# Joining pairs of groups in the routed stage of a hybrid attention and expert-retrieval block, with a rearranged front

## The chip, the cores and the metric

One core of one Trainium2 chip runs the whole layer as one launch. The metric is the time of one execution on the device in microseconds (us); lower is better. The engines are named as in the profile: PE is TensorE (matrix products), PEld its weight loads, DVE is VectorE, ACT ScalarE, POOL GpSimd and SP SyncE, which issues most DMAs. Matrix products write only to PSUM, a memory of eight banks of 512 float32 columns by 128 rows; the other tiles lie in SBUF.

## The reference

Sequence 256, model width 2048, all float32. Cut to what matters:

```python
h = x @ w_in[l]                                    # q, six k/v, gates, conv
kc, vc = compress_kv(k_c, ...), compress_kv(v_c, ...)   # 15 compressed positions
p_c = masked_softmax(q @ kc * scale - slopes * dist_c)  # "compressed scores"
o_nsa = g0 * (p_c @ vc) + g1 * o_slc + g2 * o_win       # gated branches
x = layer_norm(ALPHA * x + concat(o_nsa, o_conv) @ w_out)
# PEER: 8 heads, product keys 128 x 128 = 16384 experts
s1, s2 = q1 @ keys1, q2 @ keys2                    # per token and head
v1, i1 = top_k(s1, 16); v2, i2 = top_k(s2, 16)
top, pos = top_k(v1[:, None] + v2[None, :], 16)    # 16 of 256 candidates
eidx = i1[pos // 16] * 128 + i2[pos % 16]; g = softmax(top)
hid = gelu(sum_d(y * u_tab[eidx]))                 # 128 experts per token
out = layer_norm(ALPHA * y + sum(g * hid * v_tab[eidx]))
```

With n_slc = 4 blocks and 16 to select, all causal blocks are selected, so the selected branch is plain causal attention over all 256 positions.

## The kernel before

The kernel has five stages, and TensorE works through nearly all of them.

1. **Front.** `w_in`, `w_out` and `wq` are streamed as pieces of 1 MB (`add_piece`, `run`). Each piece is handled as two halves; each half is split into a high part `hi` (a cast on ScalarE, `high_to`, line 228) and a low part `lo` (a subtraction on VectorE or GpSimd, `low_to`, line 243), and three products of high and low parts make a float32 product (`mm3`, lines 281 to 283). Parts are made SA = 3 halves ahead of their use. Beside the pieces, generators (`conv_chain`, `compress`, `attend`, `setup_quads`) emit small instructions; a planner's clock, estimated from costs written in the code, decides after each piece of products which generator goes on (`advance`). The order is fixed when the program is built; each engine then works in order. `compressed(g)` in `attend` makes the compressed scores of a group of four heads, for the two halves of the sequence (tt) one after the other, in eight small VectorE operations each; `put` transposes them.
2. **Query stage.** For each of the 8 heads, `wq` gives the queries, `wq_keys` the scores, `shortlist` the best 16 on each side (VectorE: max, max_index, match_replace, and a cast of the indices, line 1025), and for the first REARLY = 2 heads `route_steps` joins the sides to 16 of 256 candidates (lines 1034 to 1065). Of each low part of `wq`, 2/8 are made on VectorE and 6/8 on GpSimd (WQDVE = 2).
3. **Dense U stage.** For all 16384 experts the product of the first 1024 columns of `u_tab` with y is made on TensorE and kept in `W` (128 x 256 x 128). For the other 1024 columns only the selected rows are fetched, one gather of 128 rows by GpSimd (line 1104) and one product with sum per 128 (token, expert) pairs (a "dot", line 1115). 56 dots or so are left for the next stage.
4. **Routed stage** (lines 1496 to 1756). The 256 tokens form NQ = 64 groups of four. *Extraction* of a group (`ext_hot`, `ext`, `ext_max`) picks the 128 selected values of each token out of `W`: a small bf16 product of features gives squared distances (`ho`, line 1549), a relu on ScalarE makes them one-hot (`pt`), a second small product writes a mask of -2^100 into a bank (`xp`, line 1557), four float32 products (two records each, line 1559) add the picked rows of W to it, and a maximum on VectorE (line 1564) keeps the value. *Scatter* of a group (`sc_hot`, `sc_val`, `sc`) does the reverse with the gated activations: two small products (`pp`, line 1590), a relu on ScalarE (`oh`, line 1593), a product on VectorE (`oa`, line 1600), four float32 products (`sp`, line 1606) and a copy into `W` on ScalarE (line 1608). The rows of features lie in four ranges of 32 partitions: R1 at 0, RT at 32, RX at 64, R0 at 96. One loop of NQ + LAG = 99 steps runs extraction of group q and scatter of group q - LAG (LAG = 35), written out by hand; so 34 steps have extraction alone, 30 both (the first of them only the scatter's small products), 35 scatter alone. Six PSUM banks serve it: three for small products, two for `xp`, one for `sp`. In the same loop the last gathered rows are dotted: `x_dots` issues as many gathers as a pacing formula allows, VectorE takes two dots of three, and for every third (XPOOL) GpSimd makes the product (line 1668) and ScalarE, two steps later, the sum (line 1678, `x_sum`). `weight_sums`, `weight_gelu`, `weight_gates` and `weight_rows` turn the values of half the tokens into weights, in the middle and at the end.
5. **V stage.** `W`, now the weights, times all of `v_tab` (line 1646 on), with the first 576 columns by gathers; then the second norm.

The loop's extraction step, as it stands:

```python
            if q < NQ:
                ext(q)
                pace = q + 1 + PACE * max(0, q - LAG)
                x_dots(q, min(2 * P, i0 + -(-u_left * pace // (NQ - 4 + PACE * (NQ - 4 - LAG)))))
```

## Time and profile before

| what | us |
|---|---|
| median of 3 runs (1711.64 to 1719.06) | 1715.94 |
| profiled execution, own time | 1719.01 |
| its span, first to last instruction | 1717.2 |
| TensorE busy in it | 1663.4 (97%) |
| VectorE, ScalarE, GpSimd busy | 1480.4, 862.8, 831.4 |
| routed stage, first to last of its products | 182.1 |

The page gives busy time by engine; the queries of the trace cut it into stretches, list waits, and show instructions in order of time. Matmul records overlap, since they are pipelined, so the time from one start to the next says more than a duration. VectorE's busy time contains time in which an instruction was held up after its start. The granted clock of 1.00 stands for full speed.

### The profile page before, as it was taken

The page shows a single profiled execution, that of the slowest core. Times are in us where ns is not written, and L with a number is a line of the kernel's source. Part 1 is how long each engine was busy: PE and PEld are TensorE (multiplying, and loading weights), DVE is VectorE, ACT ScalarE, POOL GpSimd, SP SyncE. Part 2 cuts the span into 40 slices and gives each one's busy share as a digit, 9 for nine tenths or more (in the row PEclk, how much of TensorE's full clock was granted, in tenths as well). Part 3 has the DMA queues.
Part 4 walks back from the last instruction along what each step waited for, and adds up shares of the span by engine and source line. Part 5 has one row for each costly group of instructions (what it writes and reads, how often), then busy time and mean ns, then how long its engine had stood idle before and what let it go on. Part 6 is the DMA issues. An engine that isn't in the chain of part 4 may idle for free.

```text
span 1717.2 us, 30946 instructions
## 1 busy us (share of the span) xinstructions
PE 1663.4 (97%) x11611; PEld 1513.9 (88%) x11611; DVE 1480.4 (86%) x2763; ACT 862.8 (50%) x1331; POOL 831.4 (48%) x650
## 2 busy tenths in 40 slices
PE   8999999999999999999899999999999999999995
PEld 8998988888999999999899987877888888888884
DVE  6988567756899999999899888865999999999998
ACT  4445666645324444444444546767545555545552
POOL 1874000064663333333333356851766666666664
PEclk9999999999999999999999999999999999999998
DMA  8764435366658999999899987762999999999996
GB/s 273 235 211 138 143 123 173 99 208 190 206 174 309 344 351 347 338 357 348 302 346 355 347 294 220 251 217 73 338 342 341 335 339 347 340 346 339 332 346 238
DMA packets 176592, 470.25 MB, mean 274 GB/s; under 512 B 17891, under 2 KB 85147, under 8 KB 176186
## 3 DMA queue, kind: packets, MB, share of 16 engines
q1 hardware_dynamic: 115680, 257.58, 44.0%
q0 software_dynamic: 57344, 209.75, 34.1%
q8 instruction: 91, 1.49, 0.3%
q10 hardware_dynamic: 3418, 0.94, 0.2%
q14 instruction: 59, 0.48, 0.1%
HBM read 463.36 MB, written 4.85 MB: 273 GB/s over the span
## 4 chain that ended last, share of the span: by engine, by line
PE 69%; DVE 14%; DMA 7%; issue 4%; ACT 3%; POOL 2%; DVEq 0%; SPq 0%; POOLq 0%; ACTq 0%
PE f L282 7%; PE f L281 7%; PE f L283 7%; DMA gv<-in_peer_v_dram,e 5%; PE hp L283 5%; PE hp L281 5%; PE hp L282 5%; PE ut L1171 4%; DVE gu L1115 4%; PE sp L1606 3%; PE xp L1559 3%; DVE ul L1175 2%; DVE lo L243 1%; POOL gu L1104 1%; PE pcg L282 1%
## 5 line engine op out<-in xcount | busy, mean ns | idle before, releaser
L1620 POOL DMA_INDIRECT gv<-in_peer_v_dram,e x256 | 347.7, 1358 | 200.3 <-DVE gacc L1777 154.3
L1104 POOL DMA_INDIRECT gu<-in_peer_u_dram,eu x202 | 193.0, 956 | 330.2 <-DVE gu L1115 245.0
L281 PE MATMUL hp<-yh,uh 128*128 128x256 f32 x1024 | 311.0, 304 | 0.4 <-ACT W L1417 0.3
L282 PE MATMUL f<-vl,wh 128*128 128x512 f32 (+1 forms) x768 | 293.4, 382 | 1.9 <-DVE vl L1646 1.9
L281 PE MATMUL f<-vh,wh 128*128 128x512 f32 (+1 forms) x768 | 294.0, 383 | 0.0
L283 PE MATMUL f<-vh,wl 128*128 128x512 f32 (+1 forms) x768 | 293.0, 382 | 0.0
L283 PE MATMUL hp<-yh,ul 128*128 128x256 f32 x1024 | 290.6, 284 | 0.5 <-DVE ul L1175 0.4
L282 PE MATMUL hp<-yl,uh 128*128 128x256 f32 x1024 | 289.7, 283 | 0.0
L1174 ACT ACTIVATE uh<-ut 128x512 fp32r<-128x512 f32 x256 | 152.7, 598 | 263.5 <-PE ut L1171 257.0
L1646 DVE TENSOR_TENSOR vl<-vr,vh 128x1472 fp32r<-128x1472 f32 x127 | 215.0, 1693 | 33.3 <-ACT vh L1645 33.3
L243 POOL TENSOR_TENSOR lo<-raw,hi 128x1024 fp32r<-128x1024 f32 (+2 forms) x83 | 172.9, 2097 | 129.8 <-ACT hi L228 128.7
L1115 DVE SCALAR_TENSOR_TENSOR gu<-gu,yp 128x1024 f32<-128x1024 f32 x193 | 229.3, 1212 | 2.5 <-DMA gu<-in_peer_u_dram,eu 2.2
L228 ACT ACTIVATE hi<-raw 128x1024 fp32r<-128x1024 f32 (+1 forms) x138 | 142.5, 1037 | 156.8 <-PE pwq L282 41.0
L1634 ACT ACTIVATE wh<-W 128x256 fp32r<-128x256 f32 (+1 forms) x129 | 86.7, 673 | 244.3 <-PE f L282 244.3
L1777 DVE SCALAR_TENSOR_TENSOR gacc<-gv,hv,gacc 128x576 f32<-128x576 f32 x256 | 197.3, 812 | 0.2 <-DMA gv<-in_peer_v_dram,e 0.2
L281 PEld LDWEIGHTS hp<-yh,uh 128*128 128x128 f32 x1024 | 196.5, 192 | 0.8 <-ACT W L1417 0.8
L282 PEld LDWEIGHTS hp<-yl,uh 128*128 128x128 f32 x1024 | 197.1, 192 | 0.0
L283 PEld LDWEIGHTS hp<-yh,ul 128*128 128x128 f32 x1024 | 196.0, 191 | 1.2 <-DVE ul L1175 1.0
L1175 DVE TENSOR_TENSOR ul<-ut,uh 128x512 fp32r<-128x512 f32 x256 | 167.1, 681 | 21.9 <-ACT uh L1174 21.4
L1645 ACT ACTIVATE vh<-vr 128x1472 fp32r<-128x1472 f32 x127 | 180.7, 1423 | 0.0
L282 PEld LDWEIGHTS f<-vl,wh 128*128 128x128 f32 x768 | 144.2, 188 | 26.6 <-DVE vl L1646 2.6
L283 PEld LDWEIGHTS f<-vh,wl 128*128 128x128 f32 x768 | 144.2, 188 | 24.9
(374 smaller groups left out, 3730.4 us busy)
## 6 DMA issues: line engine op xcount, KB each, us to landing
vr<-in_peer_v_dram SPq DMA_DIRECT2D x128, 736.0 KB
ur<-in_peer_u_dram SPq DMA_DIRECT2D x128, 512.0 KB
raw<-in_w_in_dram SPq DMA_DIRECT2D x32, 1024.0 KB
raw<-in_w_out_dram SPq DMA_DIRECT2D x16, 1024.0 KB
raw<-in_peer_wq_dram SPq DMA_DIRECT2D x15, 1024.0 KB
gv<-in_peer_v_dram,e POOLq DMA_INDIRECT x256, 7.0
gu<-in_peer_u_dram,eu POOLq DMA_INDIRECT x202, 7.5
raw<-in_w_in_dram SPq DMA_DIRECT2D x4, 608.0 KB
```

Source lines behind the costliest of these rows:

```text
L243: e.tensor_tensor(lo[:, a:b], src[:, a:b], hi[:, a:b].bitcast(F32), op=OP.subtract)
L281: nc.tensor.matmul(acc, lhsT=ah, rhs=bh, start=start, stop=False)
L282: nc.tensor.matmul(acc, lhsT=ah, rhs=bl, start=False, stop=False)
L283: nc.tensor.matmul(acc, lhsT=al, rhs=bh, start=False, stop=stop)
L1104: nc.gpsimd.indirect_dma_start(out=gt, out_offset=None, in_=ug, in_offset=bass.IndirectOffsetOnAxis(ap=fl(eu, tt)[:, c:c + 1], axis=0))
L1115: nc.vector.scalar_tensor_tensor(gt, gt, 1.0, yr, op0=OP.mult, op1=OP.mult, accum_out=hv[:, tt, c:c + 1])
L1174: nc.scalar.activation(uh, pt, AF.Copy)
L1175: nc.vector.tensor_tensor(ul, pt, uh.bitcast(F32), op=OP.subtract)
L1620: nc.gpsimd.indirect_dma_start(out=gv[:, tt], out_offset=None, in_=v_tab, in_offset=bass.IndirectOffsetOnAxis(ap=fl(e4, tt)[:, j:j + 1], a ...
L1645: nc.scalar.activation(vh, src[:, s], AF.Copy)
L1646: (nc.gpsimd if early else nc.vector).tensor_tensor(vl, src[:, s], vh.bitcast(F32), op=OP.subtract)
L1777: nc.vector.scalar_tensor_tensor(gacc[:, tt], gv[:, tt], wv[:, tt, j:j + 1], gacc[:, tt], op0=OP.mult, op1=OP.add)
```

## The change

It has these parts:

- **Paired groups.** The first QP = 36 groups are extracted in pairs: the small products of two groups are issued together (the second group's from copies of the feature rows at RH = 96 and R1), then their eight float32 products. Then 28 steps with extraction of q and scatter of q - LAG, LAG = 37, and one step with scatter alone; then the last 36 groups are scattered in pairs, with copies of the feature rows at R2 = 32 and RX. The copy of `sp` into W goes to VectorE for every second group of the pairs. Banks and slots are named by hand instead of taken from rings: six banks, and two more in the scatter pairs. The mask's factor 2^100 moves from `quad` into the features. The loads of features, `hot_load` and `feat_load`, are issued once per copy.
- **Casts later.** The cast of the shortlist's indices moves from VectorE to ScalarE, and is issued one head later.
- **One engine per low part.** Of the four halves of a head of `wq`, three low parts are made whole on GpSimd and the fourth on VectorE.
- **Routing in one bank.** For the two early heads the candidates and one-hot products lie in one PSUM bank; ScalarE copies one operand there, and one more reduction writes a copy of i1. The scores of `wq_keys` go round three banks instead of two.
- **Merged compressed scores.** Both halves of the sequence in one set of operations of twice the size; for the first group the banks come from the ring "S".
- **Front.** Low parts are issued after the last `advance` of a half while the planner is in its "quiet" phase (instead of before it), loads of pos and w2 move to the start of `compress`, a guessed cost in `conv_norm` changes, and each next set of compressed scores starts when qT's copy is due.

Cut to what matters:

```diff
-LAGX = 3
+QP = 36
-    taps = const.tile([64, P], BF, name="taps")
-    R1, RT, RX, R0 = slice(0, 20), slice(32, 37), slice(64, 84), slice(96, 116)
+    taps = const.tile([P, P], BF, name="taps")
+    R1, R2, RX, R0 = (slice(a, a + 20) for a in (0, 32, 64, 96))
+    RT, RH = slice(32, 37), slice(96, 101)
...
-                    if j == (len(subs[s]) - 1 if quiet() else len(subs[s]) // 2):
+                    if j == len(subs[s]) // 2 and not quiet():
                         low_to(u + ahead)
                     advance()
+                low_to(u + ahead)
...
+        for nm, pos, w2 in (("k", pos_k, w2_k), ("v", pos_v, w2_v)):
+            w2s[nm] = wk.tile([P, 2, HD], F32, name=f"w2{nm}", tag="w2")
+            nc.scalar.dma_start(w2s[nm], w2[0].rearrange("(c p) d -> p c d", p=P))
+            pns[nm] = wk.tile([16, P], F32, name=f"pn{nm}", tag="pn")
+            nc.scalar.dma_start(pns[nm], pos[0].rearrange("(l r) d -> l (r d)", r=2))
...
+            def begin():
+                c4 = [(psb.tile([P, 512], F32, name=f"cs{g}{half}", tag="S") if g == 0 else turn_tile(f"cs{g}{half}"))
+                      [:, :4 * NCMP].rearrange("p (t h c) -> p t h c", t=2, h=2) for half in range(2)]
...
                 side = compressed(u // per + 1)
+                yield box["qt"]
...
-        add_cols(wq, h * 256, yt, f"pwq{h}", WQDVE if h else 0, lambda a, h=h: accq.__setitem__(h, a))
+        add_cols(wq, h * 256, yt, f"pwq{h}", (0, 0, 0, 8) if h else 0, lambda a, h=h: accq.__setitem__(h, a))
...
-        nc.vector.tensor_copy(f12s[:, :, h], x12)
+        casts[h] = lambda: nc.scalar.activation(f12s[:, :, h], x12, AF.Copy)
...
+        if banked:
+            bank = psb.tile([P, 512], F32, name=f"cand{h}{tt}", tag="T", bufs=1)
+            other = bank[:, T:]
+            cand = flat3(bank, TOPK, TOPK)
+            first = other[:, :TOPK]
+            nc.scalar.activation(first, v12[:, 0], AF.Copy)
+            i1p, efp = (bank[:, i * TOPK:(i + 1) * TOPK] for i in range(2))
+            yield
...
+    def ext_hot(q, pair=False):
+        hp, r = (banks[q % 2], (RT, RH)[q % 2]) if pair else (banks[2], RT)
+        nc.tensor.matmul(hp, lhsT=taps[r], rhs=bts[q // NB][r, :, q % NB], start=True, stop=True)
+        return hp
...
+    def ext_mask(q, pair=False):
+        xps[q], r = (banks[2 + q % 4], (RX, R1)[q % 2]) if pair else (banks[3 + q % 2], RX)
+        nc.tensor.matmul(xps[q], lhsT=frow["ext", q // NB][r, q % NB], rhs=quad[r], start=True, stop=False)
...
+    def sc_hot(m, pair=False):
+        o = 2 * (m % 2) if pair else 0
+        for n, (which, r) in enumerate(((1, R2), (0, RX)) if o else ((1, R1), (0, R0))):
...
+        for q in range(0, QP, 2):
+            loads(q)
+            loads(q + 1)
+            hps_ = [ext_hot(p, True) for p in (q + 2, q + 3)]
+            for p in (q, q + 1):
+                ext_mask(p, True)
+            if q:
+                ext_max(q - 2)
                 ext_max(q - 1)
...
+            for p, hp in zip((q + 2, q + 3), hps_):
+                ext_relu(p, hp, True)
+            for p in (q, q + 1):
+                ext(p)
+                x_dots(p, due(p))
...
+        for m in range(NQ - QP, NQ, 2):
+            loads(m + LAG)
+            loads(m + LAG + 1)
+            nxt = [p for p in (m + 2, m + 3) if p < NQ]
+            for p in nxt:
+                sc_hot(p, True)
+            if m == NQ - QP:
+                weight_gates(1)
+            for p in nxt:
+                sc_relu(p, True)
+            for p in nxt:
+                sc_val(p, True)
+            sps = [sc(p, True) for p in (m, m + 1)]
+            for p, sp in zip((m, m + 1), sps):
+                sc_keep(p, sp, p % 2 == 1)
```

## Rows read from the trace of the kernel before

**Rows 1.** The page, part 1: busy time, share of the span, instructions.

```profile
PE 1663.4 (97%) x11611; PEld 1513.9 (88%) x11611; DVE 1480.4 (86%) x2763; ACT 862.8 (50%) x1331; POOL 831.4 (48%) x650
```

**Rows 2.** Stretches: length, busy by engine (count), granted clock, DMA share, GB/s.

```profile
437.00:510.00 73.00, 69.27 (x567) 68.86 (x566) 71.88 (x253) 23.62 (x25) 49.69 (x30) 0.98 0.57 188
...
1005.60:1055.70 50.10, 49.81 (x344) 36.49 (x343) 39.45 (x65) 28.05 (x49) 34.91 (x30) 1.00 0.79 260
1055.70:1137.90 82.20, 76.21 (x594) 63.05 (x593) 69.72 (x116) 57.90 (x111) 60.57 (x47) 0.94 0.73 236
1137.90:1187.70 49.80, 49.20 (x352) 37.13 (x351) 24.64 (x38) 38.19 (x72) 9.13 (x10) 1.00 0.31 103
```

**Rows 3.** Waits of TensorE: total us, times, longest us.

```profile
PE pwq L283 <- DVE lo L243: 3.2, 1, 3.2
PE ho L1549 <- DVE oa L1600: 2.8, 2, 1.9
PE t L803 <- DVE sc L792: 2.5, 2, 1.4
PE cs L709 <- ACT gates L651: 2.2, 1, 2.2
...
PE ppk L571 <- DMA pnk<-in_cmp_pos_k_dram: 1.7, 1, 1.7
...
PE cs L709 <- ACT qT L662: 0.9, 1, 0.9
```

**Rows 4.** TensorE in order of time, scatter alone: start, duration, instruction.

```profile
1181.26 0.39 PE L1590 MATMUL pp<-quad,fsc 20*128 20x512 bf16 x2
1181.57 1.16 PE L1606 MATMUL sp<-oa,oh 128*128 128x128 f32 x8
1182.66 0.39 PE L1590 MATMUL pp<-quad,fsc 20*128 20x512 bf16 x2
```

**Rows 5.** TensorE in order of time, one joined step of extraction and scatter.

```profile
1068.26 0.39 PE L1590 MATMUL pp<-quad,fsc 20*128 20x512 bf16 x2
1068.27 0.38 PE L1549 MATMUL ho<-bt,taps 5*128 5x512 bf16 x1
1068.27 0.39 PE L1557 MATMUL xp<-quad,fext 20*128 20x512 bf16 x1
1068.59 1.16 PE L1559 MATMUL xp<-W,pt 128*128 128x128 f32 x8
1069.58 1.06 PE L1606 MATMUL sp<-oa,oh 128*128 128x128 f32 x8
1070.57 0.39 PE L1590 MATMUL pp<-quad,fsc 20*128 20x512 bf16 x2
```

**Rows 6.** First and last of 24 joined steps' first small products, 23 periods apart.

```profile
1065.95 0.39 PE L1590 MATMUL pp<-quad,fsc 20*128 20x512 bf16 x2
...
1123.42 0.39 PE L1590 MATMUL pp<-quad,fsc 20*128 20x512 bf16 x2
```

**Rows 7.** A stretch as in rows 2, after the wait for pnk.

```profile
92.00:97.00 5.00, 5.00 (x30) 5.00 (x31) 4.54 (x13) 1.60 (x3) 2.38 (x1) 0.66 0.99 315
```

**Rows 8.** Groups by line on VectorE, 1005.6 to 1137.9: busy us, mean ns, idle before.

```profile
L1564 DVE TENSOR_REDUCE top<-xp 128x4 f32<-128x512 f32 x64 | 44.0, 688 | 11.2 <-PE xp L1559 10.9
L1115 DVE SCALAR_TENSOR_TENSOR spare<-spare,yp 128x1024 f32<-128x1024 f32 x18 | 21.8, 1211 | 1.8 <-DMA spare<-in_peer_u_dram,eu 1.8
```

**Rows 9.** All engines in order of time near 1128; in brackets idle before, releaser.

```profile
1126.54 2.37 POOL L1668 TENSOR_TENSOR moreh<-moreh,morel 128x1024 f32<-128x1024 f32 x1
...
1128.94 1.06 ACT L1678 ACTIVATE moreh<-moreh 128x1024 f32<-128x1024 f32 x1 [2.16 <-POOL moreh L1668]
...
1130.62 1.72 PE L1606 MATMUL sp<-oa,oh 128*128 128x128 f32 x8 [1.69 <-ACT W L1608]
```

**Rows 10.** VectorE and GpSimd in order of time in the query stage, near 470.

```profile
470.00 3.95 DVE L1054 TENSOR_TENSOR oh<-fab,iota 128x256 f32<-128x256 f32 x1
...
470.00 5.66 POOL L243 TENSOR_TENSOR lo<-raw,hi 128x768 fp32r<-128x768 f32 x3
```

More of the change, by code (lines that the diff above doesn't have):

```diff
@@ L434, in setup_quads @@
         yield dv(512, pe(0.43))
-        nc.scalar.dma_start(taps[RT], quad[0:20:4, :P])
+        for r in (RT, RH):
+            nc.scalar.dma_start(taps[r], quad[0:20:4, :P])
         flags.add("quads")
@@ new lines, in compressed, with spread @@
+            sm = wk.tile([P, 2, 2, 4], F32, name=f"csm{g}", tag="csm")
+            box_ = {}
+            def spread(t):
+                return t.rearrange("p t (h o) -> p t h o", o=1).to_broadcast([P, 2, 4, NCMP])
+            def begin():
+                c4 = [(psb.tile([P, 512], F32, name=f"cs{g}{half}", tag="S") if g == 0 else turn_tile(f"cs{g}{half}"))
+                      [:, :4 * NCMP].rearrange("p (t h c) -> p t h c", t=2, h=2) for half in range(2)]
+                for tt in range(2):
+                    for hp_ in range(2):
+                        for half in range(2):
+                            b0 = half * HD
+                            nc.tensor.matmul(c4[half][:, tt, hp_], lhsT=qT[b0:b0 + HD, hp_, tt * P:(tt + 1) * P],
+                                             rhs=kc[b0:b0 + HD, g], start=True, stop=True)
+                t = pe(0.6)
@@ L1039, in route_steps @@
         yield
-        scr = tk.tile([P, T], F32, name=f"scr2{h}{tt}", tag="oh", bufs=1)
+        scr = other if banked else tk.tile([P, T], F32, name=f"scr2{h}{tt}", tag="oh", bufs=1)
         nc.vector.max_index(pos[:, :8], vals[:, :8], src)
@@ L1058, in route_steps @@
             nc.vector.tensor_reduce(dst[:, tt, h], oh, axis=AX.X, op=OP.add)
+            if s == 0 and banked:
+                nc.vector.tensor_reduce(i1p, oh, axis=AX.X, op=OP.add)
             yield
-        ef = tk.tile([P, TOPK], F32, name=f"ef{h}{tt}", tag="ef")
-        nc.vector.scalar_tensor_tensor(ef, i1[:, tt, h], float(P), i2[:, tt, h],
+        ef = efp if banked else tk.tile([P, TOPK], F32, name=f"ef{h}{tt}", tag="ef")
+        nc.vector.scalar_tensor_tensor(ef, i1p, float(P), i2[:, tt, h],
                                        op0=OP.mult, op1=OP.add)
@@ L1373, in tile_hybrid_block @@
         wq_keys(PH - 1, q0)
+        casts[PH - 2]()
         last = scratch(PH - 1)
@@ L1656, in tile_hybrid_block @@
     ups.close()
-    psx = xs.enter_context(tc.tile_pool(name="psx", bufs=3, space=PSUM, reuse_waits="tile"))
-    psp = xs.enter_context(tc.tile_pool(name="psp", bufs=1, space=PSUM, reuse_waits="tile"))
-    psp2 = None
+    psx = xs.enter_context(tc.tile_pool(name="psx", bufs=1, space=PSUM, reuse_waits="tile"))
+    banks = [psx.tile([P, 512], F32, name=f"bank{i}") for i in range(6)]
+    slots_ = [px.tile([P, 512], F32, name=f"slot{i}", bufs=1) for i in range(7)]
+    more_banks, more_slots = [], []
     late = []
@@ L1696, in tile_hybrid_block, with due, loads @@
     with tc.manual_schedule():
-        ext_hot(0)
-        ext_hot(1)
+        for q in range(2):
+            ext_relu(q, ext_hot(q, True), True)
         u_left = 2 * P - issued
         i0 = issued
-        for q in range(NQ + LAG):
+        def due(q):
+            pace = q + 1 + PACE * max(0, q - LAG)
+            return min(2 * P, i0 + -(-u_left * pace // (NQ - 4 + PACE * (NQ - 4 - LAG))))
+        def loads(q):
             m = q - LAG
@@ L1721, in tile_hybrid_block @@
             if q == NQ // 2:
                 weight_sums(0)
-            if q < NQ:
+            for p, hp in zip((q + 2, q + 3), hps_):
[3 more added lines that the diff above has]
+                x_dots(p, due(p))
+            if q == NQ // 2:
+                weight_gelu(0)
+        for q in range(QP, NQ + 1):
+            m = q - LAG
+            loads(q)
+            if q < NQ:
+                sc_hot(m + 1)
+                sc_relu(m + 1)
+            else:
+                more_slots = [px.tile([P, 4 * NB * P], BF, name="slot7", tag="bt").bitcast(F32)[:, :512]]
+                for p in (m + 1, m + 2):
+                    sc_hot(p, True)
+                    sc_relu(p, True)
+            for p in range(q - 2 if q == QP else q - 1, q):
+                ext_max(p)
+            if q + 2 < NQ:
+                ext_relu(q + 2, ext_hot(q + 2))
+            if q < NQ:
+                sc_val(m + 1)
+                ext_mask(q)
@@ L1724, in tile_hybrid_block @@
                 ext(q)
-                pace = q + 1 + PACE * max(0, q - LAG)
-                x_dots(q, min(2 * P, i0 + -(-u_left * pace // (NQ - 4 + PACE * (NQ - 4 - LAG)))))
-            if q == NQ:
+                x_dots(q, due(q))
+            else:
+                for p in (m + 1, m + 2):
+                    sc_val(p, True)
                 while done < 2 * P:
```

212 lines of the change are left out of this document (101 added, 111 removed).

## The prediction

> **What bounds the kernel now.** I read the page first: TensorE is busy 97% of the span [rows 1]. A change off TensorE's path can therefore only fill its holes, or shorten what TensorE itself needs. So I cut the span into stages. The routed stage is three stretches: extraction of groups alone (50.10 us), extraction and scatter joined (82.20), scatter alone (49.80); together 182.1 us, and in none of them is VectorE, ScalarE or GpSimd fuller than TensorE [rows 2]. Then I listed who made TensorE wait [rows 3], and last I read its order of time in that stage.
>
> There the reader is to see two periods. A group alone takes 1.40 us from one pair of small bf16 matmuls to the next: 0.31 until the eight fp32 records begin, 1.09 until the next small ones [rows 4]. Where extraction and scatter run joined, all four small matmuls start within 0.01 us of each other, in four row groups of the array, and two groups together take 2.31 us [rows 5]. Two groups alone would take 2.81. So a joint round, with one set of small matmuls and one change back to them for two groups, saves 0.50 us.
>
> A second thing to see is what a wait costs beyond itself. After the 1.7 us wait for pnk, the window from 92 to 97 us shows TensorE always busy at a mean granted clock of 0.66, a mix of its 2.4 and 1.2 GHz levels: 5.0 x 0.34 = 1.7 us lost on top [rows 3, 7].
>
> **The change part by part.** I make the sum against the profiled run, 1719.0 us; it was 3.1 above the median of the runs shown, and I take the same off at the end.
>
> *Paired groups.* Before, 34 groups are extracted alone, one more step has only the scatter's small matmuls with it, 29 steps are joined, and 35 scatter alone: 70 x 1.405 + 29 x 2.31 = 165.3 us of TensorE work. The stage took 182.1, so 16.8 us are waits, slow clock and the start. After, there are 18 extraction pairs, one step with only the scatter's small matmuls, 27 joined steps, one scatter alone, and 18 scatter pairs: 2 x 1.405 + 63 x 2.31 = 148.3. The gain is 17.0 us, if the pairs hold 2.31. The pairs use the same four row groups, two of them with copies of the same rows (R2, RH), so I take the overlap that the joined steps show.
>
> Do the other engines hold it? An extraction pair puts on VectorE two maxima of 0.69 and the share of the gathered dots, at 1.21 each [rows 8]. By the pacing formula a pair asks for as many gathered rows as a joined step does today, and a joined step too has two VectorE operations on 512 columns of PSUM, one of them this maximum. The joined steps from 1065.95 to 1123.42 are 23 periods in 57.47 us, 2.50 each, one long stall among them [rows 6]. So I charge the 18 extraction pairs 0.19 us each, 3.4, or 45.0 us in all. VectorE's 39.45 us of work for 34 groups [rows 2] would be 41.8 for the 36: it fits, but barely. The lone groups already had 50.1 - 34 x 1.405 = 2.3 us of waits and start, most of which the 3.4 replace: net 1.1, and I take 2 for the shorter leads told below. In a scatter pair VectorE has two products and now one copy, all on 512 columns of PSUM; at the maximum's 0.69 each that is 2.1 us against 2.31; ScalarE has three operations instead of four. TensorE stays last, by 0.2 us; I charge nothing and keep 18 x 0.2 = 3.6 us as the bound. The 16.8 us of old waits I leave, since the 27 joined steps keep their order, banks and queues. **Routed stage: -15**, bounds -17 (no new wait) and -4 (extraction pairs gain nothing, -9, and scatter pairs lose 3.6).
>
> *What the pairs move and add.* Each load of the small features is issued twice on SP in the paired stretches, and must land within two pairs (4.6 us) where it had four groups (5.6). Behind it on SP are only the next such loads and, once, the first rows of V. If one lands late, TensorE waits in that round, at about the price of the stall in rows 9. The sum of an even GpSimd product on ScalarE is issued two groups later as before, but that is now one pair: 2.3 us instead of 2.8, against a product of 2.37 [rows 9]. Queued behind that sum on ScalarE are the next pair's two relus, and TensorE waits for those. Such a wait as it is today: at 1128.94 ScalarE had waited 2.16 us for GpSimd, and TensorE then 1.69 us for ScalarE [rows 9].
>
> *The front.* Loads of pnk and w2 are issued at the start of the stream: the wait of 1.7 and the slow clock of 1.7 behind it go, -3.4. They are four issues more ahead of ScalarE's early casts, which run three half pieces ahead of TensorE; that lead hides them. Compressed scores of the first group take their banks from another ring, so that they don't wait for the gates, and the others start only when qT has been cast: 2.2 and 0.9, -3.1 [rows 3]. The merged scores halve the number of small VectorE operations, which TensorE doesn't wait for today; nothing. In the query stage the 3.2 us wait for a low part on VectorE goes together with the slow clock behind it, -4.9, if what delayed VectorE goes. What delayed it is plain: an is_equal of 256 elements took 3.95 us while GpSimd ran its low parts back to back [rows 10]; VectorE is "busy" 71.88 of 73 us there, TensorE 69.27 [rows 2]. The change puts one operand of each such step into PSUM and the casts on ScalarE.
>
> The Trainium skill (SBUF — State Buffer, Who interferes with whom) says that a VectorE instruction with two SBUF inputs and a GpSimd instruction that reads SBUF exclude each other for a whole instruction, and one with at most one SBUF input doesn't. By that rule the steps in PSUM are free of it, as assumed; but the new whole low part on VectorE still has two SBUF inputs, and by the rule each of its seven could wait a GpSimd part out: the front's gain would be 4.9 smaller.
>
> The new wait in the query stage: VectorE's first step of a banked head waits for a small ScalarE copy, which is queued behind casts that wait for TensorE to free their buffers. Behind it on VectorE are the shortlist and the next low part, and TensorE waits for that part only three half pieces later. That lead hides it; if it doesn't, each of the two heads costs what the old stall cost, 4.9.
>
> The front's instructions are put in order by the planner's clocks, so new waits will appear where none were. Those that it leaves are of 0.9 to 2.8 us [rows 3]; I take one with its slow clock, 3.4, off the 11.4. **Front: -8**, bounds -13 and 0. Extra rows of quad, scaled features, a second copy of taps and loads moved earlier are small work on VectorE and queues that hold nothing up; TensorE's stretches before the routed stage and after it are untouched.
>
> **Sum:** 1719.0 - 15 - 8 = 1696.0 in the profiled run's terms; less 3.1, 1693 us.
>
> **Rivals.** (a) *Gathers and evacuation pace the pairs.* The Trainium skill (TensorEngine Tiling (Array Packing), PSUM Bottleneck) warns that after tiling the copies out of PSUM may become the bottleneck, and advises using ScalarE and VectorE both; the scatter pairs do the latter, the extraction pairs don't. From the rows: VectorE has 39.45 us of work in the first 50.1 already, and 41.8 for 36 groups against the pairs' 41.6 without a wait. If extraction pairs stay at 2.8, 9 us go: -6 - 8, 1702. Against it speak the 23 joined periods, which hold 2.50 with as many such operations each [rows 6]. (b) *The front gives it back.* Waits move instead of vanishing: only -15 is left, 1701. (c) *The pairs don't overlap*: four small matmuls run two by two, about 0.3 us a round, 36 rounds, 11 us: 1704. The start times in rows 5 speak against it. (d) *Slower: ScalarE waits for GpSimd's products in every round.* The place is the sum behind each of some 17 products, the price what rows 9 show, 1.69 plus 1.7 of slow clock, 3.4 us each. All 17 would cost 58 us: 1751. It ends slower than before if more than 7 of them hit (23 / 3.4), and slower by 0.5% from 10 on. Against it: ScalarE has 28.05 us of work in the first 50.10 [rows 2], so that a short wait is absorbed.
>
> **How the numbers follow.** Forecast 0.50, (a) 0.22, (b) 0.15, (c) 0.04, (d) 0.06, and 0.03 for something else that is harmless. I predict 1693. The range takes in -17 and -13 (1686, and 2 for the spread of the runs) at the low end, and at the high end (a), (b) and (c) and a mix of them: 1684 to 1709. A measurement of this kernel can tell about 0.5% from no change, 8.6 us: faster means below 1707.4. Forecast, (a), (b) and (c) lie there with some of each reaching over the bound: faster 0.83, same 0.11, slower 0.06.
>
> **What would show it.** Pairs right: the first and third stretch show rounds of 2.31 us with four small matmuls starting together, and the stage is near 167 us. Rounds of 2.5 and more with VectorE or ScalarE named before TensorE mean (a); small matmuls that start 0.3 us apart mean (c); ScalarE waiting for GpSimd again and again means (d). Front right: no wait for pnk, gates or the query's low part, no 3.95 us is_equal, and the dense U stage begins about 8 us earlier. If its start is unmoved, (b). The prediction is wrong if the routed stage gains under 6 us or the front loses.

## The result and the profile after

The changed kernel takes 1703.51 us (median of 6 runs, 1699.98 to 1706.22) where the kernel before takes 1716.04 in the runs beside it: a ratio of 0.9926, 95% interval 0.9909 to 0.9943, some 12.5 us or 0.74% faster. A second set of runs gave 0.9917 (0.9900 to 0.9933). That is faster by more than 0.5%, inside the range of 1684 to 1709, and 10.5 us above the 1693 that was predicted. The profiled executions are 19.0 us apart (1719.01 and 1699.98), more than the medians, so the two traces alone overstate the change.

The main stretches, each from its first TensorE instruction to that of the next, in us of the profiled executions; "again" is a second trace of the same kernel:

| stretch | before | before again | after | after again |
|---|---|---|---|---|
| start to first key product of the compression (pck) | 111.5 | 111.5 | 108.1 | 108.2 |
| pck to first query product (pq) | 77.8 | 77.8 | 78.2 | 78.1 |
| attention and mixing: pq to first product of the query stage (pwq) | 216.1 | 217.6 | 224.1 | 224.7 |
| query stage: pwq to the first transposition of U | 104.2 | 104.2 | 98.4 | 98.5 |
| dense U stage | 496.0 | 493.2 | 490.8 | 490.7 |
| routed stage | 182.1 | 183.0 | 168.1 | 174.8 |
| V stage and end | 529.5 | 529.6 | 530.4 | 530.2 |
| span | 1717.2 | 1716.8 | 1698.2 | 1705.2 |

Part 1 of the page of after, which answers rows 1:

```profile
PE 1647.9 (97%) x11611; PEld 1508.8 (89%) x11611; DVE 1473.5 (87%) x2726; ACT 854.1 (50%) x1319; POOL 829.1 (49%) x643
```

Two paired rounds of extraction in after, TensorE in order of time (start, duration, instruction), which answer rows 4 and 5:

```profile
1006.08 0.39 PE L1586 MATMUL bank<-bt,taps 5*128 5x512 bf16 x2
1006.09 0.39 PE L1595 MATMUL bank<-quad,fext 20*128 20x512 bf16 x2
1006.41 2.05 PE L1600 MATMUL bank<-W,slot 128*128 128x128 f32 x16
1008.39 0.39 PE L1586 MATMUL bank<-bt,taps 5*128 5x512 bf16 x2
```

All four small matmuls start within 0.01 us, sixteen fp32 products follow, and the next round begins 2.31 us after the last. The three parts of the routed stage of after (extraction pairs, joined steps, scatter pairs), columns as in rows 2:

```profile
999.63:1046.57 46.94, 44.34 (x365) 36.08 (x365) 41.47 (x71) 29.02 (x52) 36.71 (x31) 1.00 0.89 297
1046.57:1120.00 73.43, 69.23 (x553) 57.37 (x553) 63.82 (x108) 53.83 (x105) 56.69 (x44) 0.95 0.75 249
1120.00:1167.77 47.77, 45.49 (x372) 38.40 (x371) 34.69 (x57) 32.04 (x59) 11.01 (x12) 0.96 0.34 114
```

The first part holds 36 groups in less time than 34 took before (50.10, rows 2). The last part holds 36 in place of 35, but took only 2 us less than before (49.80). The waits of TensorE in after, the largest and the largest for loads, which answer rows 3:

```profile
PE t L811 <- DVE sc L800: 10.0, 3, 4.9
PE f L287 <- DVE vl L1693: 2.5, 3, 1.2
PE bank L1647 <- ACT W L1655: 2.4, 2, 1.6
PE yt L1281 <- DVE part L1261: 1.9, 1, 1.9
PE bank L1629 <- DVE slot L1641: 1.8, 3, 1.3
...
PE ut L1198 <- DMA ur<-in_peer_u_dram: 1.2, 1, 1.2
...
PE bank L1629 <- DMA fsc<-feat: 1.0, 1, 1.0
```

The waits for pnk, gates, qT and the query's low part on VectorE are gone. In their place stands one that was 2.5 us in rows 3 and is 10.0 now: the transposition t of the attention waits for VectorE's weighted scores (sc, line 800). This is where the expected gain of the front went. The rows on TensorE, VectorE and ScalarE around the first of these waits that bear on it, in order of time; in brackets idle time before and what ended it:

```profile
228.48 0.28 PE L288 MATMUL pq<-xh,lo 128*128 128x256 f32 x1
228.70 1.07 PE L721 MATMUL cs<-kc,qT 64*128 64x15 f32 x16
229.61 0.68 PE L770 MATMUL s<-kds,qT 64*128 64x256 f32 x4
229.80 0.35 DVE L726 TENSOR_TENSOR csb<-cs,bc 128x60 f32<-128x60 f32 x2 [3.78 <-PE cs L721]
...
230.80 0.92 PE L811 MATMUL t<-ident,sc 128*128 128x128 f32 x4
...
232.81 0.49 PE L770 MATMUL s<-kdw,qT 64*128 64x128 f32 x3
...
233.82 0.51 ACT L788 ACTIVATE sc<-sc,st 128x256 f32<-128x256 f32 x1 [2.07 <-DVE st L780]
...
236.06 0.29 ACT L732 ACTIVATE csb<-csb 128x120 f32<-128x120 f32 x1
236.39 0.28 DVE L736 TENSOR_REDUCE csm<-csb 128x8 f32<-128x120 f32 x1 [2.10 <-ACT csb L732]
...
237.74 1.14 DVE L800 TENSOR_SCALAR sc<-sc,st 128x256 f32<-128x256 f32 x4
238.15 1.11 PE L811 MATMUL t<-ident,sc 128*128 128x128 f32 x4 [4.85 <-DVE sc L800]
238.91 0.56 PE L286 MATMUL pq<-xh,hi 128*128 128x256 f32 x1
```

Between 228.48 and 238.91 no dense product pq is issued. Compressed scores, scores, transpositions and the next scores follow each other, and then TensorE has nothing left. The exponential of the compressed scores (ACT L732) stands behind four exponentials of the scores; VectorE's scaling of them (L736) has to wait 2.10 us for it; the weighing (L800), which has nothing to do with the compressed scores, stands behind that scaling, and t behind the weighing. Of the 4.85 us, the scaling accounts for 1.44: the last sum of the exponentials that the weighing needs is read at 235.90, and its first step starts at 237.34. For the rest TensorE waits for the maxima and exponentials of the scores themselves, because no dense product is left to fill the time. And the products after the wait run almost all at the lower level of the clock, 1.2 GHz: 4.85 us at a mean of 0.53, 2.3 us lost on top (columns as in rows 2).

```profile
238.15:243.00 4.85, 4.85 (x26) 4.63 (x28) 4.11 (x12) 3.24 (x11) 0.00 (x0) 0.53 0.08 17
```

### The profile page after: what moved, and what is told of

Same layout as the page of the kernel before. It is cut to its first block, busy times and chain, and to the rows that moved or that the text cites. A ratio compares the mean times of both kernels' runs of the same rounds, so it can differ in the third digit from the quotient of the medians.

```text
span 1698.2 us, 30783 instructions
## 1 busy us (share of the span) xinstructions
PE 1647.9 (97%) x11611; PEld 1508.8 (89%) x11611; DVE 1473.5 (87%) x2726; ACT 854.1 (50%) x1319; POOL 829.1 (49%) x643
## 3 DMA queue, kind: packets, MB, share of 16 engines
HBM read 464.12 MB, written 4.85 MB: 276 GB/s over the span
## 5 line engine op out<-in xcount | busy, mean ns | idle before, releaser
L247 POOL TENSOR_TENSOR lo<-raw,hi 128x1024 fp32r<-128x1024 f32 (+1 forms) x76 | 173.0, 2290 | 125.6 <-ACT hi L229 119.5
L286 PEld LDWEIGHTS f<-vh,wh 128*128 128x128 f32 x768 | 144.2, 188 | 24.8 <-ACT vh L1692 0.3
```

What stands on the lines that cost most here:

```text
L247: e.tensor_tensor(lo[:, a:b], src[:, a:b], hi[:, a:b].bitcast(F32), op=OP.subtract)
L286: nc.tensor.matmul(acc, lhsT=ah, rhs=bh, start=start, stop=False)
```

## The experiments

Each time is given as its ratio to the kernel before on the same chip, with the 95% interval; a gain in us is worked out from that ratio, and lengths of stretches are from one profiled execution each.

**Pairs alone, and front alone.** The change divided in two, both against the kernel before. The first kernel takes the edits of the routed stage with the constants and features that it needs (first diff, cut to its core), the second all the others (second diff):

```diff
-LAGX = 3
+QP = 36
...
-    taps = const.tile([64, P], BF, name="taps")
+    taps = const.tile([P, P], BF, name="taps")
...
+        for q in range(0, QP, 2):
+            loads(q)
+            loads(q + 1)
+            hps_ = [ext_hot(p, True) for p in (q + 2, q + 3)]
...
```

```diff
+                low_to(u + ahead)
...
-        yield dv(2048) + 1.5
+        yield engine("v", 3.9) + 0.3
...
+                yield box["qt"]
...
+        tag = "SSo"[h % 3]
...
```

> The kernel before with the routed stage of the change alone: paired extraction and scatter, copies of the feature rows, their loads; the front (early loads, compressed scores, query stage) is left as before. Theory 1 (the stage from the first small product to the first V product is worth 13.9 us, as the traces of before and after show, 182.1 to 168.2, and nothing else of the change is worth much): 12 to 14 us faster than before, the stage again 167 to 170 us. Rival 1 (part of those 13.9 us comes from the front, which hands the stage over in another state): the stage takes 172 us or more and the gain is under 10 us. Rival 2 (the 5.1 us that the dense U stage lost belong to the routed stage's earlier loads): U stage near 491 us and the gain near 18 us.

> The kernel before with the front of the change alone: early loads, casts on ScalarE and whole low parts in the query stage, banked routing, merged compressed scores; the routed stage is left as before. Theory 1 (the front's savings of about 3.4 and 5.8 us are given back in the attention stretch): 0 to 2 us faster than before, first U product at about 509 us, two waits of over 4 us for weigh's product there. Rival (the attention stretch's loss was a chance of one execution): 7 to 9 us faster, first U product near 501 us.

Pairs alone: 0.9966 (0.9952 to 0.9979), 5.8 us faster. Its routed stage took 170.0 us and its U stage 491.9. Front alone: 0.9990 (0.9977 to 1.0003), no difference that can be measured; the first transposition of U starts at 508.3, with the same wait as in after:

```profile
PE t L809 <- DVE sc L798: 10.0, 3, 4.9
```

So the front gives back what it saves, and the gain is the routed stage's. Theory 1 of the first run held for the stage, not for the time, which fell short of 12 to 14 us. Its second rival falls: the U stage took 491.9 us, but it took as long in front alone, where no load of the routed stage is moved, and the gain is nowhere near 18. What stayed open was why the median of pairs alone fell short of its trace.

**Pairs alone again** (the same kernel).

> The routed stage of the change alone, once more, on another chip for all I know. Its first median was 6.5 us under that of before (3.6 to 8.2), though its trace showed a routed stage of 170.0 us, 11 to 13 under those of before. Theory 1 (the traced execution was the fastest of eight; the routed stage of the others is longer, by stalls that differ from execution to execution): stage 170 to 176 us in this trace, median 6 to 11 us under before. Rival (pairs alone lose elsewhere what they gain in the routed stage, which the front of the change then mends): stage 168 to 171, another stage 3 us or more longer than in the trace of before.

0.9938 (0.9917 to 0.9959), 10.6 us faster (8.6 between the medians); routed stage 171.8, U stage 492.1, V stage 530.1, the last two no longer than in the other traces. One stretch is longer than before: the attention, 219.1 us against 216.1 and 217.6. Its waits of TensorE are the same as before to 0.1 us, but from 189 to 250 us the mean clock is 0.94 there and 1.00 in before. The pairs don't touch that code, and the first trace of pairs alone has 217.6 there, so this is chance of an execution, and the rival falls. The two sets of runs are 5.8 and 10.6 us under before; their intervals, 3.6 to 8.2 and 7.0 to 14.3 us, overlap a little.

**After without the hand-in of qT.** One line less:

```diff
                 side = compressed(u // per + 1)
-                yield box["qt"]
             beside()
```

> The kernel after without one line: each head group's generator no longer hands in the ready time of qT before its compressed scores start. Theory A (that line makes the attention steps start late, so that score, weigh and value products stand one behind the other without query products between, and TensorE waits 4.9 and 4.3 us for weigh's product): both waits go, the 8 us lost between the first query product and the first pooling product come back, and this kernel is 6 to 9 us faster than the kernel after, 20 us faster than before. Theory B (the merged compressed scores do it): within 2 us of the kernel after, both waits stay. In either case the old wait for qT's cast, 0.9 us, may come back.

**After with split compressed scores**, one query tile at a time as before, the line kept; the first group's banks go back to the old ring with it, which the cut leaves out:

```diff
-            yield begin()
-            yield power(clock)
-            yield scale()
-            if g:
-                yield clock
+            yield begin(0)
+            yield power(0, clock)
+            yield begin(1)
+            yield max(scale(0), power(1, clock))
             put(0)
...
+            yield scale(1)
             put(1)
```

> The kernel after with its compressed scores undone: one query tile at a time as before, twice as many steps of half the size; the line that hands in qT's ready time is kept. Theory A (that line is the cause of the lost 8 us): within 2 us of the kernel after, and the waits for weigh's product stay. Theory B (the merged steps put 0.5 us more in one piece before weigh's product on VectorE and are the cause): both waits go and it is 6 to 9 us faster than the kernel after. The first group's bank goes back to the old ring, so the wait for the gates, 2.2 us, may come back.

**After with both undone.**

> The kernel after with both undone: compressed scores one query tile at a time as before, and no hand-in of qT's ready time. Theory B of the last runs (the merged scores are the cause; the line adds to it): the waits for weigh's product stay as short as with split scores alone (1.1 us in all), first U product near 501 to 503, 5 to 8 us faster than the kernel after. Rival (the line was what kept the split scores in order): the wait for qT's cast, 0.9 to 2.2 us, and a wait of 2 us or more for weigh's product come back, first U product at 504 or later, and it is slower than split scores with the line.

**After again, as control.**

> The kernel after, unchanged, as the control for the runs beside it and as a second trace of it. Expected 12.5 us faster than before again (9 to 16). Theory 1 (the two waits for weigh's product belong to the kernel's order and not to one execution): both are there again, near 4.9 and 4.3 us, and the first U product starts within 1.5 us of 508.8. Rival (chance): they are gone or under 2 us, and the U stage starts before 506.

These four make almost a square; the split kernels differ in the first group's banks too. Attention and mixing, pq to pwq, in us, and the waits of t for VectorE's weighing in brackets:

| | without the line | with the line |
|---|---|---|
| split scores | 218.1 (0.2), ratio 0.9886 (0.9869 to 0.9902) | 216.9 (1.1), ratio 0.9889 (0.9862 to 0.9916) |
| merged scores | 220.2 (5.4), ratio 0.9903 (0.9882 to 0.9923) | 224.7 (10.0), ratio 0.9917 (0.9900 to 0.9933) |

The wait of 10.0 us, its largest single one 4.9, came back to the tenth in after again and in front alone: it belongs to the order of the instructions, not to one execution. Neither theory of the first two runs holds as it was put. By the lengths, merging costs in both columns (2.1 and 7.8 us); the line costs only where the scores are merged (4.5 us) and nothing where they are split (1.2 us shorter). The intervals of the four ratios overlap, so it is the lengths that carry this. Merging costs more than the table shows, because the split kernels wait 2.2 us for the gates again, which the merged ones don't: beside split scores with the other ring (212.9 us, next run) it costs 11.8 us with the line. With split scores the wait of t all but goes, with the line or without it. The two waits of the kernel with the merged scores and without the line, and the largest of the one with split scores and the line, in that stretch:

```profile
PE t L811 <- DVE sc L800: 5.4, 3, 3.2
PE cs L721 <- ACT qT L669: 2.2, 2, 1.3
```

```profile
PE cs L716 <- ACT gates L658: 2.2, 1, 2.2
PE yt L1280 <- DVE part L1260: 1.9, 1, 1.9
PE ct L748 <- DVE csm L726: 1.7, 2, 1.0
PE t L810 <- DVE sc L799: 1.1, 3, 0.7
```

That TensorE waits for the weighing with merged scores and hardly without is shown, and so is where the time goes. Before the pooling TensorE has no dense product for 10.43 us around the first of these waits in every trace with merged scores and the line (10.44 in one), for 5.67 and then 3.97 us with merged scores alone, and never for as much as 3.4 us in a trace with split scores, before included. Why the order comes out like that is only argued: a step that is handed in late has passed its planned times, after which the planner puts no dense products between its parts. No run tested the planner's clock by itself.

**Split scores, other ring.** The first group's banks as in the change, so that they don't wait for the gates:

```diff
-                c3 = [flat3(turn_tile(f"cs{g}{tt}{half}"), 2, NCMP)
-                      for half in range(2)]
+                c3 = [flat3(psb.tile([P, 512], F32, name=f"cs{g}{tt}{half}", tag="S") if g == 0
+                            else turn_tile(f"cs{g}{tt}{half}"), 2, NCMP) for half in range(2)]
```

> Split compressed scores with the line that hands in qT's ready time, as in the run of split scores, and the first group's scores take their banks from the ring that the change gave them, so that they need not wait for the gates. Theory 1 (what the change saved at the compressed scores was that wait of 2.2 us, and only the merged form gave it back): no wait for the gates, first U product near 499.5, 2 to 3 us faster than split scores alone, 1695 to 1697. Rival (the wait moves, to another wait for that bank or to the pooling's transposition): the wait is 1.5 us or more elsewhere, first U product at 501 to 503, time within 1 us of split scores alone.

The wait for the gates is gone and no other has come for it; pq to pwq takes 212.9 us, 4.0 less than with split scores alone, where the slow clock followed that wait (a mean of 0.72 from 214 to 220 us there, 1.7 us lost, and 1.00 from 210 to 216 here). First transposition of U at 497.7. 1695.14 us, ratio 0.9871 (0.9845 to 0.9897): faster than the change, whose ratios were 0.9926 and 0.9917.

**Before again.** Nothing edited.

> The kernel before, unchanged, for a second trace. Theory 1 (what the dense U stage lost in the trace of before, 3.9 us of wait for a row of U and 1.7 of slow clock behind it, is chance of an execution, and no part of the gain of the change): the U stage takes 490 to 493 us here in place of 496.0, and the routed stage 179 to 182. Rival (it belongs to the kernel before, and the change removes it): 495 to 497 again, with a wait of 3 us or more for a row of U near 820 us.

U stage 493.2, routed stage 183.0; the wait for a row of U is 2.2 us here. All other traces have 490.7 to 495.0 for the U stage, whatever was in them. So about half of the 5.2 us between the first two traces is gone in the second trace of before, and the other 2.5 us lie within the spread of the changed kernels: chance for the most part, not gain.

**Feature loads on ScalarE's queue.** The scatter pairs took 47.6 to 49.9 us in all unedited paired traces; 18 rounds of 2.31 and one group alone are 43.0. In six of the eight TensorE waited 1.0 to 2.8 us for the features fsc, whose loads stand on SP behind rows of V. SP's queue near 1130 us in the first trace of pairs alone, in order of time, and the wait on it:

```profile
1131.15 1.46 SPq L1489 DMA_DIRECT2D fsc<-feat  x4
1132.65 8.28 SPq L1635 DMA_DIRECT2D vr<-in_peer_v_dram  x2
1140.97 4.72 SPq L1489 DMA_DIRECT2D fsc<-feat  x8
```

```profile
SPq L1635 <- POOL vl L1664: 5.7, 1, 5.7
```

A row of V (line 1635) waits 5.7 us for its buffer, and the features that TensorE needs next are issued behind it; TensorE waited 2.8 us for features in that trace, once 2.3. So:

```diff
-            nc.sync.dma_start(t[r], src[:, b:b + NB])
+            (nc.scalar if use == "sc" and q >= 40 else nc.sync).dma_start(t[r], src[:, b:b + NB])
```

> The kernel after with one edit: in the scatter pairs the loads of the small features of rows 40 and on are issued on ScalarE's queue and not on SP's, where rows of V stand ahead of them, one of which waits 5.7 us for its buffer. Theory 1 (that queue makes the features late): no wait of TensorE for the features (2.1 to 2.8 us in the paired traces), the rounds of 2.8 to 4.7 us behind it are near 2.4, the 18 scatter pairs take 44 to 45 us in place of 47.8 to 50, and the kernel is 2 to 5 us faster than the kernel after. Rival (the loads are late because all 16 DMA engines are busy with rows of V, or ScalarE's four issues a round cost as much): the waits stay or move to ScalarE, and the time is within 2 us.

Ratio 0.9922 (0.9905 to 0.9938), the same as after. No wait for features, but after again on the same chip had none of note either, and the scatter pairs took 48.5 us in both. Both have two long rounds, 4.5 and 4.3 us, in the same place instead. The theory falls as put; the run didn't test what it was meant to.

**Gate rows last.** On top of that edit:

```diff
             if m == NQ - QP + 2:
-                weight_rows(1)
                 tks.close()
...
+        weight_rows(1)
     dump("wv", wv)
```

> The kernel with the moved feature loads and one more edit: the transposition and copy of the second tile's gated weights (weight_rows(1)), which stood in the third scatter pair, stands behind the last pair. Theory 1 (that step, whose transposition waits for a bank and whose copy stands ahead of the next relus on ScalarE, makes the round of 4.5 us and, by the slow clock behind it, the next of 4.3): both rounds fall to 2.3 to 2.6, the scatter pairs take 44 to 45 us in place of 48.4, 3 to 4 us faster than with the loads moved alone. Rival (VectorE and ScalarE are held there by something else, as in the joined rounds of 4 us in the same trace, where no such step stands): a round of over 4 us stays at the same place and the time is within 1.5 us.

Ratio 0.9939 (0.9918 to 0.9960): no gain. The two long rounds are 2.45 and 2.31, but now the features are late again, though ScalarE's queue has no rows of V:

```profile
1139.00 4.77 ACTq L1518 DMA_DIRECT2D fsc<-feat  x4
...
1140.68 0.39 PE L1629 MATMUL bank<-quad,fsc 20*128 20x512 bf16 x1 [0.88 <-DMA fsc<-feat]
...
1143.82 1.08 ACT L1635 ACTIVATE slot<-bank 128x512 f32<-128x512 f32 x2 [4.28 <-DMA fsc<-feat]
```

The four issues held ScalarE's queue for 4.77 us, and ScalarE's own next step with it for 4.28. The issues themselves are short. The second and the third, taken out of that row, are 0.28 us each:

```profile
1141.18 0.28 ACTq L1518 DMA_DIRECT2D fsc<-feat  x1
1143.11 0.28 ACTq L1518 DMA_DIRECT2D fsc<-feat  x1
```

The rest of the 4.77 us is two waits. Each of these loads uses the semaphore that a row of V, issued on SP at 1130.56 and 1131.75, used before it, and it starts 0.02 us after that row's last update, at 1141.16 and 1143.09. So a load on a queue without rows of V still waited until a row of V had landed. The scatter pairs took 50.3 us. Late features are thus no matter of SP's queue alone. Whether the round of 4.5 us is gone for the moved rows can't be read from this run: on this chip the kernels that kept them (pairs alone again, split scores with the other ring) had 2.56 there.

**Features earlier**, on split scores with the other ring:

```diff
-            if m + 6 >= 0 and (m + 6) % NB == 0 and m + 6 < NQ:
-                feat_load("sc", m + 6, ...
+            for r in ([m + 6] if m + 6 < 36 else []) + ([m + 12] if m + 12 >= 36 else []):
+                if r >= 0 and r % NB == 0 and r < NQ:
+                    feat_load("sc", r, ...
...
+                    tag="fext" if use == "sc" and q in (36, 40, 52, 56) else f"f{use}")
```

> The kernel of the last split-score run (split scores, first group's banks from the other ring) with one edit in the routed stage: features of rows 36 and on are loaded 12 groups ahead instead of 6, still on SP, every second pair of rows into the two buffers that the extraction's features no longer need. Theory 1 (features are late because they are issued only three pairs, 6.9 us, ahead, when all DMA engines are busy with rows of V; another queue could not help that): TensorE waits under 0.5 us in all for features (2.2 in the trace without the edit), the two rounds around each such wait fall from 2.8 to 3.9 us to 2.3 to 2.5, the scatter pairs take 44 to 45 us in place of 47.6, and the time is 2 to 4 us lower, 1691 to 1693. Rival (what the pairs wait for is the evacuation and the gate steps between them, and the late features only stand where that wait would stand anyway): scatter pairs 47 us or more, time within 1.5 us of the run without the edit.

By the order of the code the small products read the features two rounds after their loads are issued, 4.6 us as the prediction had it and not three pairs, and five rounds after with the edit. Ratio 0.9861 (0.9837 to 0.9885), not told apart from the 0.9871 without the edit. No wait for features, and from 1130.21 on 13 rounds in a row of 2.31 us. But the scatter pairs took 49.2 us: the two long rounds are back (5.03 and 4.79 us), with VectorE and ScalarE both standing still before them. TensorE, ScalarE and VectorE there:

```profile
1120.86 2.05 PE L1646 MATMUL bank<-slot,slot 128*128 128x128 f32 x16
...
1124.37 1.08 ACT L1634 ACTIVATE slot<-bank 128x512 f32<-128x512 f32 x2 [3.77 <-PE bank L1646]
1124.41 0.69 DVE L1652 COPY W<-bank 128x512 f32<-128x512 f32 x1 [3.90 <-remote]
...
1125.16 0.33 PE L1578 MATMUL bank<-ident,gs 128*128 128x128 f32 x1 [2.24 <-DVE W L1652]
...
1126.86 3.42 PE L1646 MATMUL bank<-slot,slot 128*128 128x128 f32 x16
```

Both engines start again within 0.04 us of each other, 1.5 us after the last product before that had ended by its modelled end (1120.86 + 2.05). The record of semaphores tells what they waited for: TensorE's signals. Seven of its products, ending from 1120.46 to 1122.91, signal their end, and all seven signals are recorded in one burst from 1124.32 to 1124.64. In after again, neither and feature loads moved the same place has 4.2 to 5.0 us with no signal of TensorE, where six or seven were due. These traces and before again are also the only ones in which signals of TensorE lack a record at all, 76 to 93 of some 1250 each. Why the signals came late stays open. TensorE then waits for VectorE in the transposition of the gate rows, and its next products run at the slow clock (3.42 us for 2.05). The length of the stretch was thus much the same in each run (48.5, 50.3 and 49.2 us), but not for the same cause: late features where the long rounds were absent, long rounds where the features were in time. With those two rounds at 2.31 us the stretch here would be 44.0 us (49.2 - 9.8 + 4.6, an estimate from this trace), as theory 1 had it; no run shows it, and both edits at once weren't tried.

## Why the prediction was right and where it was wrong

**The paired rounds: right.** Most of them take 2.31 us with four small matmuls at once, as read off the joined steps. Eighteen extraction pairs were put at 45.0 us; from the first small matmuls of a full round to the first joined step they took 45.1 (1001.47 to 1046.57) in after, and 44.9 to 47.8 in the other unedited paired traces, 45.9 on average. That the charge of 0.19 a round came out is in part luck: it isn't spread over the rounds, but lies in a few of 2.8 to 3.5 us. Rivals (a) and (c) fall. So does (d): ScalarE's waits for GpSimd's products in the routed stage of after are 10.2 us in all, and TensorE's rounds hold beside them.

**The scatter pairs: the term that was too small.** "I charge nothing and keep 18 x 0.2 = 3.6 us as the bound." Most rounds are indeed 2.31, but the stretch took 47.6 to 49.9 us in the eight paired traces with this order, 48.3 on average, against the 43.0 charged: 5.3 us more, past the bound. The cost was not in every round but in four to seven. The first, which scatters one group alone and holds `weight_sums`, takes 3.1 us in every trace where 1.4 was charged. The others have late features, the steps of the gates and gate rows or TensorE's late signals, and the slow clock behind. The prediction had named the late load, and set it at no cost. It had the rows of V behind the loads on SP; in the first trace of pairs alone one stands ahead of them.

**The routed stage.** Put at -15, it gained 14.0 between the first two traces, 8.2 between the second two. All eight unedited paired traces average 171.1 us, the three unpaired ones (before twice, front alone) 181.5: 10.4. Besides the scatter pairs, the start cost 1.0 us more (1.8 to the first full round, against 0.8), which the sum hadn't. The joined steps gained 1.2 beyond the two rounds that they have less (75.0 us for 28 rounds, 80.8 for 30). What varies in them is an old stall. Each of the eight traces has one joined round of 4.4 to 7.8 us, in which TensorE waits 1.3 to 3.3 us for VectorE's product, and in seven of them VectorE had waited 1.7 to 3.5 us for a gathered row. Before has such a round too, of 6.1 us. Here is the longest, in after without the hand-in of qT:

```profile
1087.55 1.22 DVE L1140 SCALAR_TENSOR_TENSOR spare<-spare,yp 128x1024 f32<-128x1024 f32 x1 [3.43 <-DMA spare<-in_peer_u_dram,eu]
...
1090.04 0.58 PE L1628 MATMUL bank<-quad,fsc 20*128 20x512 bf16 x1 [3.20 <-DVE slot L1640]
```

So gathers do hold up the joined steps, as rival (a) had it for the pairs, where they don't.

**The front: wrong, by the step on the merged scores.** Of "-8", the first term (pnk, -3.4) measured 3.3 between the first two traces, and 3.0 by the first query product, since the next stretch is 0.3 longer. The query stage was put at -4.9 and gained 5.8 in every trace with its edits; which of these edits did it wasn't tested. What was predicted for its cause shows too. The step that took 3.95 us in rows 10 has one operand in PSUM now, and its kind takes 0.43 on average, where the four of before took 1.31. The whole low parts on VectorE take twice as long beside GpSimd in the query stage (first row, 430 to 512 us) as in the attention (second row, 186 to 286 us), where GpSimd has none to make:

```profile
L247 DVE TENSOR_TENSOR lo<-raw,hi 128x1024 fp32r<-128x1024 f32 x6 | 15.7, 2613 | 1.9 <-ACT hi L229 1.9
L1078 DVE TENSOR_TENSOR cand<-cand,iota 128x256 f32<-128x256 f32 x4 | 1.7, 429 | 0.1
```

```profile
L247 DVE TENSOR_TENSOR lo<-raw,hi 128x1024 fp32r<-128x1024 f32 x15 | 18.2, 1220 | 4.8 <-ACT hi L229 4.8
```

The rule of the Trainium skill (SBUF — State Buffer, Who interferes with whom), that a VectorE instruction with two SBUF inputs and a GpSimd one that reads SBUF exclude each other, agrees with that: the six parts take 1.4 us longer each. The loss of 4.9 us that I worked out as its price didn't come, since these parts run ahead of TensorE, which waits for VectorE's low parts no more.

The failed step reads: "The merged scores halve the number of small VectorE operations, which TensorE doesn't wait for today; nothing." I counted their work and not their place. One longer chain (scores, maximum, exponential, scaling of both query tiles) has to end before VectorE goes on to the weighing behind it, and TensorE does wait for that. The planner besides put no dense products between these longer steps, as the stretch of 10.43 us shows; that its clock did so because of their length is argued. In place of the -3.1 put for the compressed scores, the attention stretch grew by 6.9 us (224.5 on average of the five traces with the change's front, 217.6 of the four with the old one). With split scores and the other ring it took 212.9: the -3.1 was there to be had, 4.7 with its slow clock. I had reserved 3.4 us for new waits that the order would bring; they cost 11.6 (224.5 less 212.9).

**The sum.** By averages over traces the front gained 1.6 (first transposition of U at 509.38 with it, 510.94 without) and the routed stage 10.4, 12.0 together, which the measured 12.5 and 14 bear out. The test that the prediction set, the start of the U stage, was 509.6 before and 508.8 after, all but unmoved: rival (b), which gave 1701, describes the outcome best, with the routed stage 4.6 us short of its term besides. The 10.5 us by which the forecast was too low are the front's 6.4 and these 4.6, 11.0 by the averages.

## What to carry to other kernels

A round read off one stage carries over to another that uses the array in the same way; what has to be priced beside it are the steps and loads that stand between the rounds, which have less time than before (4.6 us for a load of features instead of 5.6). Merging small operations on an engine that isn't the bottleneck is not free: look for what stands behind the merged chain on its engine, and for who waits for that. Take a second trace of the same kernel before a difference of 5 us in a stage of 490 is explained.

## What the runs showed of the hardware

A wait of TensorE costs more than itself, here as in the prediction: 2.3 us of slow clock behind the wait of 4.85 at 238.15, and behind one of 1.3 in the routed stage 1.7 (9 us at 0.81 from 1080 on). New to me was that a small load on ScalarE's queue can wait for a row of V on SP's, by the semaphore that the two use in turn: four issues of 0.28 to 0.34 us held ScalarE's queue for 4.77 us, after rows of V had moved at 341 to 415 GB/s from 1134 to 1140 us. And seven signals of TensorE's products were recorded up to 3.9 us late in one burst, with VectorE and ScalarE standing still for 3.9 and 3.8 us until they came; why is open.
